# Triangular inverses of both head groups on GpSimd, two key tiles ahead of the first chunk, and value centring by a matrix product

## Chip, core and metric

The kernel runs on one core of a Trainium2 chip. The metric is device microseconds of one execution; the median of three executions of the kernel before is 2632.55 us (2632.36 to 2641.84).

The core has five instruction streams that run side by side and meet through semaphores: TensorE (PE in the profile, with its weight loads as PEld), VectorE (DVE), ScalarE (ACT), GpSimd (POOL) and SyncE (SP), which issues the DMAs. Each engine works through its own queue strictly in order. In this kernel TensorE reads SBUF and writes PSUM, and GpSimd works on SBUF alone.

## The reference, cut to what matters

A network of three layers on 512 tokens of width 1024 in fp32. Only the first mixer, a gated delta-rule recurrence with 16 heads of 64 channels, is touched by the change:

```python
def rwkv7_step(S, inp):
    r_t, dec_t, k_t, v_t, kk_t, a_t = inp
    sa = jnp.einsum('bhij,bhj->bhi', S, -kk_t)
    S = (S * dec_t[:, :, None, :] + sa[..., None] * (kk_t * a_t)[:, :, None, :]
         + v_t[..., None] * k_t[:, :, None, :])
    y = jnp.einsum('bhij,bhj->bhi', S, r_t)
    return S, y
...
    _, y = lax.scan(rwkv7_step, S0, seq)
    m = jnp.mean(y, axis=-1, keepdims=True)
    var = jnp.mean(jnp.square(y - m), axis=-1, keepdims=True)
    y = ((y - m) * lax.rsqrt(var + GN_EPS)).reshape(B, T, D) * ln_g + ln_b
    ...
    bonus = (jnp.sum(rh * kh * r_k, axis=-1, keepdims=True) * vh).reshape(B, T, D)
    out = ((y + bonus) * g).astype(h.dtype) @ w_o
```

The mean over a head's 64 value channels is taken off y. The recurrence is linear in v, so the kernel takes that mean off v before the recurrence instead. The cross attention that follows needs keys and values of a 256-token memory (`mem`), for layer 0 and, later, for layer 1.

## The kernel before, in words

Activations are kept with features on partitions and 512 tokens on the free axis, as eight tiles of 128x512. Weights stream from HBM through two raw buffers (`wraw`, line 41 on) in one fixed order, given by `rw_keys` and its fellows. Most are split into a high and a low part (ScalarE copy, line 63; VectorE or GpSimd subtraction, line 64) and used in three fp32r products (lines 221 to 223). The layer-1 memory keys are not split: one fp32 product each (line 219), straight out of the raw buffer, which is held until the last of the eight products of a tile.

The recurrence is computed in chunks of 64 tokens. The eight feature tiles are two groups of four (g = 0 and 1), and a group is worked off in eight chunks. For one group:

- `key_norms(g)` and `decays(g)` make the norms of the keys and the decays; `scaled(p, ...)` for the group's four tiles makes the scaled keys and queries, and the blocks of a 32x32 strictly triangular system into `qall`, which is `inv[g]`. Its products go through the two `aux` banks of PSUM.
- `inverse32(inv[g], outer)` inverts all these triangular systems at once: it transposes `qall` into `al` on VectorE, builds the inverse in `xl`, and transposes back into `qall`. With `outer` (group 0) it does this by 31 rank-one updates on GpSimd, a product (line 1337) and a sum (line 1338) each. Without it (group 1) it works on VectorE in two 16-row halves and a coupling block (lines 1346 to 1361).
- `prepare(g, n)` makes what chunk n needs without the state: products of keys and queries (line 1389), masked by VectorE (1391), transposes (1395), the inverse of the 64x64 system out of the 32x32 ones (lines 1402 to 1416, with one GpSimd product at 1413), and for every even n `values(g, n)`: transposes of v to tokens (1370), the mean over 64 channels (1373, 1374) and its subtraction (1379), the last three on VectorE.
- `advance(g, n, ...)` carries the state through chunk n: products at 1433, 1441, 1444, 1452 and 1470, with ScalarE and VectorE copies between, and one GpSimd product (1465).

`chunks(g, extra)` runs step n as prepare(n), advance(n - 2), extra(n). For group 0, `extra` is `others`, which does the work of group 1 beside it, by the string `BESIDE[n]`: "a" is key_norms and decays of group 1, a digit 4 to 7 is `scaled` of that tile, "i" the inverse of group 1, a letter A to H a `bonus` (two GpSimd products at line 1271, a head sum on TensorE by lines 1083 and 1084, and a row at 1091). `SPARE` says how many steps of the layer-1 memory keys (one product of line 219 a step, 64 in all) each of the three places in `advance` takes. The layer-0 memory keys follow in group 1; the parts that they need are put where the inverse's tiles lay.

The order of each queue is fixed ahead of the run. A planner places the instructions by its own estimate of their times, with program order as the priority among those that it holds ready; `issue_after` adds an order by hand. So an instruction early in the program can be queued behind a later one.

Of the kernel before, what the change touches and what calls it, by code (L numbers as in the profile page):

```python
# [11 lines left out]
ALU = mybir.AluOpType  # L12
# [83 lines left out]
class Net:  # L96
# [945 lines left out]
    def rwkv_masks(self, pool, scratch):  # L1042
# [13 lines left out]
        self.mlt, self.bd32 = z(32, "mlt"), z(64, "bd32")  # L1056
        nc.gpsimd.memset(self.bd32, 0.0)
# [54 lines left out]
    def rwkv(self, g_next, after):  # L1112
# [210 lines left out]
        def inverse32(qall, outer):  # L1323


            fl = lambda t: t.rearrange("p a b -> p (a b)")
            tmp = tp1.tile([P, 4, T], F32, tag="sig", name=self.nm("inv"))
            al = tp1.tile([P, 32, 32], F32, tag="ee", bufs=2, name=self.nm("al"))
            xl, pr = tmp[:, :2].rearrange("p a (b s) -> p (a b) s", s=32), tmp[:, 2:].rearrange("p a b -> p (a b)")
            nc.vector.transpose(fl(al), fl(qall))  # L1330
            nc.gpsimd.memset(xl, 1.0)
            nc.gpsimd.affine_select(out=xl, in_=xl, compare_op=ALU.is_equal, fill=0.0, base=0, pattern=[[1, 32], [-1, 32]], channel_multiplier=0)
            if outer:

                for k in range(31):
                    o = pr[:, : (31 - k) * (k + 1)].rearrange("p (t s) -> p t s", s=k + 1)
                    PT(out=o, in0=bc(al[:, k + 1 :, k : k + 1], [P, 31 - k, k + 1]), in1=bc(xl[:, k : k + 1, : k + 1], [P, 31 - k, k + 1]), op=ALU.mult)  # L1337
                    PT(out=xl[:, k + 1 :, : k + 1], in0=xl[:, k + 1 :, : k + 1], in1=o, op=ALU.add)  # L1338
                nc.vector.transpose(fl(qall), fl(xl))
                return  # L1340

            for t in range(1, 16):
                o = pr[:, : 2 * t * t].rearrange("p (b s k) -> p b s k", b=2, s=t)
                for b in range(2):
                    c = slice(16 * b, 16 * b + t)
                    TT(out=o[:, b], in0=xl[:, c, c].rearrange("p k s -> p s k"), in1=bc(al[:, 16 * b + t : 16 * b + t + 1, c], [P, t, t]), op=ALU.mult)
                for b in range(2):
                    nc.vector.tensor_reduce(out=xl[:, 16 * b + t, 16 * b : 16 * b + t], in_=o[:, b], axis=AX.X, op=ALU.add)

            m = self.t512("u", 3)[:, :256].rearrange("p (t s) -> p t s", s=16)  # L1350
            for s in range(0, 16, 4):
                o = pr[:, : 64 * (16 - s)].rearrange("p (t s k) -> p t s k", t=16, s=4)
                TT(out=o, in0=bc(xl[:, s:16, s : s + 4].rearrange("p k (t s) -> p t s k", t=1), [P, 16, 4, 16 - s]),
                   in1=bc(al[:, 16:, s:16].rearrange("p t (s k) -> p t s k", s=1), [P, 16, 4, 16 - s]), op=ALU.mult)
                nc.vector.tensor_reduce(out=m[:, :, s : s + 4], in_=o, axis=AX.X, op=ALU.add)
            for t in range(0, 16, 4):
                n = t + 4
                o = pr[:, : 64 * n].rearrange("p (t s k) -> p t s k", t=4, s=16)
                TT(out=o, in0=bc(m[:, :n].rearrange("p k (t s) -> p t s k", t=1), [P, 4, 16, n]),
                   in1=bc(xl[:, 16 + t : 20 + t, 16 : 16 + n].rearrange("p t (s k) -> p t s k", s=1), [P, 4, 16, n]), op=ALU.mult)  # L1360
                nc.vector.tensor_reduce(out=xl[:, 16 + t : 20 + t, :16], in_=o, axis=AX.X, op=ALU.add)
            nc.vector.transpose(fl(qall), fl(xl))
# [3 lines left out]
        def values(g, n):  # L1366

            ps = self.mm()
            for j in range(4):
                nc.tensor.transpose(ps[:, j * P : (j + 1) * P], vv[:, 4 * g + j, n * 64 : n * 64 + P], self.ident)  # L1370
            pv = ps.rearrange("p (j h i) -> p j h i", j=4, h=2)
            mean = self.small(8, "mv")
            nc.vector.tensor_reduce(out=mean, in_=ps.rearrange("p (a i) -> p a i", i=64), axis=AX.X, op=ALU.add)
            TS(out=mean, in0=mean, scalar1=1.0 / 64, scalar2=None, op0=ALU.mult)
            mean = mean.rearrange("p (j h) -> p j h", h=2)
            for c in range(2):
                uv = tp.tile([P, 2, 4, 64], F32, tag="uv", bufs=4, name=self.nm("uv"))
                for hh in range(2):
                    TT(out=uv[H[hh], hh], in0=pv[H[c], :, hh], in1=bc(mean[H[c], :, hh : hh + 1], [64, 4, 64]), op=ALU.subtract)
# [123 lines left out]
        inverse32(inv[0], True)  # L1503
# [14 lines left out]
        def others(n):  # L1518

            for c in BESIDE[n] if n < len(BESIDE) else ():  # L1520
# [3 lines left out]
                elif c == "i":  # L1524
                    inverse32(inv[1], False)
# [5 lines left out]
        def spare(i, ins):  # L1531
            with tc.issue_after(ins):
                for _, advance.km in zip(range(SPARE[i]), advance.keys):
                    pass
# [3 lines left out]
        advance.keys = self.memory_keys(1, 1, self.keys1)  # L1538
        chunks(0, others)
# [5 lines left out]
        advance.keys = keys = self.memory_keys(0, 1)  # L1545

# [88 lines left out]
BESIDE = "a", "457", "6F", "Di", "AGCBEH"  # L1635
# [43 lines left out]
def rw_keys():  # L1679
    al = lambda n: [(n, m, 0, KD) for m in range(KD)]  # L1680
    return (al("rw_k")[:6] + [("rw_a1", 0, 0, KD)] + al("rw_k")[6:] + [("rw_a2", 0, 0, KD), ("rw_w1", 0, 0, KD)] + [("rw_g1", j, 0, KD) for j in range(2)]
            + [("rw_w2", 0, 0, 1)] + al("rw_r")[4:] + al("rw_r")[:4] + al("rw_v") + [("rw_w2", 0, 1, 2)] + kv_keys(1)[:KD] + kv_keys(0) + [("rw_g2", j, 0, KD) for j in range(2)] + al("rw_o"))
# [98 lines left out]
```

## Time and profile before

| | |
|---|---|
| median of three executions | 2632.55 us |
| the profiled execution, its time | 2631.13 us |
| its span in the profile | 2629.4 us |
| TensorE busy | 2516.1 us (96%), mean granted clock 0.968 |
| VectorE busy | 1458.8 us (55%) |
| ScalarE busy | 1068.1 us (41%) |
| GpSimd busy | 363.3 us (14%) |

The shares are means over a long run of stages that differ. The stage of the change reaches from about 190 us, where the inverse of group 0 starts, to about 480 us, where the last chunk of group 1 ends. Of that stage the views by windows, by queue in order of time, and by line are read. In a view by windows each engine has its busy time and, in brackets, its instructions; PEclk is the granted clock of TensorE as a share of full speed (2.4 GHz). In an answer by line, three durations with slashes are the least, the median and the largest, in ns.

### The profile page before, as it was taken

How to read it: one execution, taken by the hardware profiler on the slowest of the kernel's cores; microseconds unless marked ns; L12 is line 12 of the kernel's file. 1: busy time of each engine (PE TensorE's matmuls, PEld its weight loads, DVE VectorE, ACT ScalarE, POOL GpSimd, SP SyncE). 2: the span in 40 equal slices, each digit the busy share in tenths (PEclk: the TensorE clock that was granted, in tenths of full speed). 3: DMA queues.
4: the chain of work that ended last, by engine and by line, in shares of the span. 5: the costliest groups of instructions: out<-in, count | busy, mean ns of one | idle time of the engine just before them, and what ended most of it. 6: DMA issues, size and time to landing. Idle time of an engine off the chain costs nothing.

```text
span 2629.4 us, 33965 instructions
## 1 busy us (share of the span) xinstructions
PE 2516.1 (96%) x13560; PEld 1980.9 (75%) x13560; DVE 1458.8 (55%) x2134; ACT 1068.1 (41%) x1717; POOL 363.3 (14%) x362
## 2 busy tenths in 40 slices
PE   6998989899999999999999999999999999999998
PEld 5666767687888888754788888888776778888886
DVE  7673886655577743322564877434324556555522
ACT  7844445534344432412443444333223444333321
POOL 3035532430100001100202000001010000000000
PEclk9998988899999999999999999999998999999999
DMA  3211111332232233442322322332211113222232
GB/s 127 72 49 43 34 50 41 103 104 65 81 104 97 96 92 100 129 114 81 104 65 73 105 96 97 95 90 75 72 65 41 56 37 116 94 95 95 94 96 80
DMA packets 69597, 218.36 MB, mean 83 GB/s; under 512 B 9227, under 2 KB 14748, under 8 KB 69438
## 3 DMA queue, kind: packets, MB, share of 16 engines
q1 hardware_dynamic: 69438, 216.19, 26.2%
q8 instruction: 106, 1.74, 0.3%
q14 instruction: 53, 0.43, 0.1%
HBM read 205.69 MB, written 2.10 MB: 79 GB/s over the span
## 4 chain that ended last, share of the span: by engine, by line
PE 84%; DVE 9%; ACT 2%; POOL 2%; issue 2%; DMA 0%; DVEq 0%; POOLq 0%; ACTq 0%
PE mm L221 24%; PE mm L222 24%; PE mm L223 24%; PE aux L614 2%; PE aux L324 1%; PE mm L219 1%; POOL inv L1337 1%; POOL inv L1338 1%; DVE u L1177 1%; ACT wh L63 1%; DVE wl L64 1%; PE mm L1011 1%; DVE h L1307 1%; PE aux L984 0%; PE aux L1005 0%
## 5 line engine op out<-in xcount | busy, mean ns | idle before, releaser
L63 ACT ACTIVATE wh<-wr 128x1024 fp32r<-128x1024 f32 (+5 forms) x382 | 388.0, 1019 | 753.1 <-PE mm L222 585.0
L64 DVE TENSOR_TENSOR wl<-wr,wh 128x1024 fp32r<-128x1024 f32 (+3 forms) x341 | 402.8, 1183 | 261.2 <-ACT wh L63 252.2
L222 PE MATMUL mm<-al,wh 128*128 128x512 f32 x1088 | 428.1, 394 | 2.4 <-DVE al L249 2.4
L221 PE MATMUL mm<-ah,wh 128*128 128x512 f32 x1088 | 427.9, 394 | 0.9 <-ACT wh L63 0.8
L223 PE MATMUL mm<-ah,wl 128*128 128x512 f32 x1088 | 422.7, 390 | 0.5 <-DVE wl L64 0.5
L221 PE MATMUL mm<-bh,wh 128*128 128x512 f32 (+1 forms) x1000 | 396.0, 397 | 0.1
L222 PE MATMUL mm<-bl,wh 128*128 128x512 f32 (+1 forms) x1000 | 393.5, 394 | 0.0
L223 PE MATMUL mm<-bh,wl 128*128 128x512 f32 (+1 forms) x1000 | 392.9, 395 | 0.3 <-DVE wl L64 0.3
L221 PEld LDWEIGHTS mm<-ah,wh 128*128 128x128 f32 x1088 | 204.3, 188 | 51.8 <-ACT wh L63 3.5
L223 PEld LDWEIGHTS mm<-ah,wl 128*128 128x128 f32 x1088 | 204.3, 188 | 46.6 <-DVE wl L64 2.3
L222 PEld LDWEIGHTS mm<-al,wh 128*128 128x128 f32 x1088 | 204.5, 188 | 45.7 <-DVE al L249 3.0
L272 POOL TENSOR_TENSOR acc<-acc,sq 128x512 f32<-128x512 f32 x55 | 88.4, 1608 | 981.5 <-ACT sq L271 981.2
L223 PEld LDWEIGHTS mm<-bh,wl 128*128 128x128 f32 (+1 forms) x1000 | 188.3, 188 | 44.7 <-DVE wl L64 1.2
L221 PEld LDWEIGHTS mm<-bh,wh 128*128 128x128 f32 (+1 forms) x1000 | 188.6, 189 | 42.5 <-issue 1.3
L222 PEld LDWEIGHTS mm<-bl,wh 128*128 128x128 f32 (+1 forms) x1000 | 188.5, 189 | 41.9 <-issue 0.7
L384 DVE TENSOR_TENSOR u<-mm,rs 128x512 f32<-128x512 f32 x132 | 90.5, 688 | 168.0 <-PE mm L223 167.9
L64 POOL TENSOR_TENSOR wl<-wr,wh 128x1024 fp32r<-128x1024 f32 (+2 forms) x41 | 99.2, 2423 | 588.7 <-ACT wh L63 586.4
L369 DVE TENSOR_TENSOR x<-x,mm 128x512 f32<-128x512 f32 x56 | 38.4, 686 | 137.0 <-PE mm L223 137.0
L221 PE MATMUL mm<-mh,wh 128*128 128x512 f32 (+1 forms) x224 | 87.6, 413 | 6.3 <-ACT mh L248 4.7
L222 PE MATMUL mm<-ml,wh 128*128 128x512 f32 (+1 forms) x224 | 91.5, 409 | 1.3 <-DVE ml L249 1.3
L223 PE MATMUL mm<-mh,wl 128*128 128x512 f32 (+1 forms) x224 | 90.1, 405 | 1.0 <-DVE wl L64 1.0
L398 ACT ACTIVATE uy<-uy 128x512 f32<-128x512 f32 x66 | 41.6, 631 | 120.3 <-DVE uy L396 120.2
(492 smaller groups left out, 3986.9 us busy)
## 6 DMA issues: line engine op xcount, KB each, us to landing
wr<-ffn_w_in SPq DMA_DIRECT2D x132, 512.0 KB, 3.4
wr<-ffn_w_out SPq DMA_DIRECT2D x48, 448.0 KB, 3.3
wr<-ffn_w_out SPq DMA_DIRECT2D x24, 512.0 KB, 3.5
wr<-hy_g SPq DMA_DIRECT2D x20, 512.0 KB, 3.4
wr<-kv_k SPq DMA_DIRECT2D x16, 512.0 KB, 3.5
wr<-kv_v SPq DMA_DIRECT2D x16, 512.0 KB, 3.5
wr<-xattn_w_q SPq DMA_DIRECT2D x16, 512.0 KB, 3.4
wr<-xattn_w_o SPq DMA_DIRECT2D x16, 512.0 KB, 3.4
```

What stands on the lines that cost most here:

```text
L63: self.last_hi = self.nc.scalar.activation(out=hi[:r, :c], in_=t[:r, :c], func=AF.Copy).ins
L64: (self.nc.gpsimd if i in W_POOL else self.nc.vector).tensor_tensor(out=lo[:r, :c], in0=t[:r, :c], in1=f32(hi[:r, :c]), op=ALU.subtract)
L219: self.last_mm = mm(out, lhsT=w[0], rhs=x[0], start=first, stop=last).ins
L221: mm(out, lhsT=w[0], rhs=x[0], start=first, stop=False)
L222: mm(out, lhsT=w[0], rhs=x[1], start=False, stop=False)
L223: mm(out, lhsT=w[1], rhs=x[0], start=False, stop=last)
L272: nc.gpsimd.tensor_tensor(out=self.sq, in0=self.sq, in1=s, op=ALU.add)
L324: self.last_bcast = self.nc.tensor.matmul(ps[:, b * P : (b + 1) * P], lhsT=col[:, b : b + 1].to_broadcast([P, P]), rhs=self.ident, start=T ...
L369: self.nc.vector.tensor_tensor(out=self.x[m], in0=self.x[m], in1=ps, op=ALU.add)
L384: nc.vector.tensor_tensor(out=u, in0=ps, in1=rs, op=ALU.mult)
L398: self.last_silu = nc.scalar.activation(out=y, in_=y, func=AF.Silu if l < 2 else AF.Gelu_apprx_tanh).ins
L614: nc.tensor.matmul(ps[32 * g : 32 * g + 32, 4 * e :], lhsT=w[:, 8 * g + e], rhs=t[:, g, : T - 4 * e], start=(e == 0), stop=(e == 7), skip_ ...
```

## The change

`values` replaces the four transposes of an even chunk by four products with a fixed 128x128 matrix `cen`, which is the identity less 1/64 in each of its two diagonal 64x64 blocks. The result has tokens on partitions and the mean already taken off, and ScalarE copies it (four copies of 64x256) where VectorE reduced, scaled and subtracted. `cen` is made once on VectorE.

`inverse32` loses the VectorE form: both groups take the 31 rank-one updates on GpSimd.

Sixteen steps (two tiles) of the layer-1 memory keys are issued ahead of the first chunk, and the three places in `advance` take 2, 2, 2 in group 0 instead of 3, 3, 2. Two weight tiles of the keys are moved ahead of the second half of `rw_w2` (which `decays(1)` uses) in the order of the weight DMAs. `BESIDE` has `scaled` of tile 4 in step 0, tiles 5, 6 and 7 in step 1, the inverse in step 2 ahead of bonus F, and D alone in step 3.

```diff
+        self.cen = z(P, "cen")
+        nc.vector.tensor_copy(self.cen, self.ident)
+        for h in range(2):
+            r = slice(64 * h, 64 * h + 64)
+            nc.vector.tensor_scalar(out=self.cen[r, r], in0=self.cen[r, r], scalar1=1.0 / 64, scalar2=None, op0=ALU.subtract)
...
-        def inverse32(qall, outer):
+        def inverse32(qall):
...
-            if outer:
-                for k in range(31):
-                    o = pr[:, : (31 - k) * (k + 1)].rearrange("p (t s) -> p t s", s=k + 1)
-                    PT(out=o, in0=bc(al[:, k + 1 :, k : k + 1], [P, 31 - k, k + 1]), in1=bc(xl[:, k : k + 1, : k + 1], [P, 31 - k, k + 1]), op=ALU.mult)
-                    PT(out=xl[:, k + 1 :, : k + 1], in0=xl[:, k + 1 :, : k + 1], in1=o, op=ALU.add)
-                nc.vector.transpose(fl(qall), fl(xl))
-                return
-            for t in range(1, 16):
...
-                nc.vector.tensor_reduce(out=xl[:, 16 + t : 20 + t, :16], in_=o, axis=AX.X, op=ALU.add)
+            for k in range(31):
+                o = pr[:, : (31 - k) * (k + 1)].rearrange("p (t s) -> p t s", s=k + 1)
+                PT(out=o, in0=bc(al[:, k + 1 :, k : k + 1], [P, 31 - k, k + 1]), in1=bc(xl[:, k : k + 1, : k + 1], [P, 31 - k, k + 1]), op=ALU.mult)
+                PT(out=xl[:, k + 1 :, : k + 1], in0=xl[:, k + 1 :, : k + 1], in1=o, op=ALU.add)
             nc.vector.transpose(fl(qall), fl(xl))
...
-                nc.tensor.transpose(ps[:, j * P : (j + 1) * P], vv[:, 4 * g + j, n * 64 : n * 64 + P], self.ident)
+                mmul(ps[:, j * P : (j + 1) * P], lhsT=vv[:, 4 * g + j, n * 64 : n * 64 + P], rhs=self.cen, start=True, stop=True)
             pv = ps.rearrange("p (j h i) -> p j h i", j=4, h=2)
-            mean = self.small(8, "mv")
-            nc.vector.tensor_reduce(out=mean, in_=ps.rearrange("p (a i) -> p a i", i=64), axis=AX.X, op=ALU.add)
-            TS(out=mean, in0=mean, scalar1=1.0 / 64, scalar2=None, op0=ALU.mult)
-            mean = mean.rearrange("p (j h) -> p j h", h=2)
...
-                    TT(out=uv[H[hh], hh], in0=pv[H[c], :, hh], in1=bc(mean[H[c], :, hh : hh + 1], [64, 4, 64]), op=ALU.subtract)
+                    copy(uv[H[hh], hh], pv[H[c], :, hh])
...
-                for _, advance.km in zip(range(SPARE[i]), advance.keys):
+                for _, advance.km in zip(range(spare.n[i]), advance.keys):
...
+        for _ in zip(range(16), advance.keys):
+            pass
+        spare.n = 2, 2, 2
         chunks(0, others)
...
+        spare.n = SPARE
...
-BESIDE = "a", "457", "6F", "Di", "AGCBEH"
+BESIDE = "a4", "567", "iF", "D", "AGCBEH"
...
-            + [("rw_w2", 0, 0, 1)] + al("rw_r")[4:] + al("rw_r")[:4] + al("rw_v") + [("rw_w2", 0, 1, 2)] + kv_keys(1)[:KD] + kv_keys(0) + [("rw_g2", j, 0, KD) for j in range(2)] + al("rw_o"))
+            + [("rw_w2", 0, 0, 1)] + al("rw_r")[4:] + al("rw_r")[:4] + al("rw_v") + kv_keys(1)[:2] + [("rw_w2", 0, 1, 2)] + kv_keys(1)[2:KD] + kv_keys(0) + [("rw_g2", j, 0, KD) for j in range(2)] + al("rw_o"))
```

## Rows read from the trace of the kernel before

**Rows 1.** By windows: length, PE, PEld, DVE, ACT, POOL, clock, DMA share, GB/s.

```profile
230.00:240.00 10.00, 1.73 (x33) 1.26 (x32) 6.62 (x16) 3.12 (x8) 7.48 (x18) 0.72 0.00 0
240.00:260.00 20.00, 17.46 (x104) 12.91 (x105) 7.55 (x15) 11.64 (x21) 1.67 (x3) 0.59 0.00 1
260.00:300.00 40.00, 35.29 (x501) 27.81 (x500) 30.93 (x48) 18.98 (x51) 20.64 (x18) 0.81 0.06 18
300.00:310.00 10.00, 9.80 (x181) 7.87 (x177) 9.84 (x16) 4.02 (x10) 9.63 (x8) 1.00 0.11 44
310.00:376.00 66.00, 53.06 (x602) 40.38 (x603) 63.72 (x134) 32.32 (x74) 26.46 (x22) 0.91 0.13 41
396.00:480.00 84.00, 79.32 (x1051) 65.31 (x1048) 54.76 (x96) 45.67 (x104) 24.15 (x17) 0.90 0.12 39
```

**Rows 2.** Timeline of TensorE: start, us, instructions, wait before and its releaser.

```profile
238.78 0.64 PE L1406 MATMUL mm<-xb,am 32*32 32x32 f32 x16 [5.45 <-DVE xb L1402]
278.61 3.72 PE L219 MATMUL mm<-mn,wr 128*128 128x256 f32 x16
385.68 0.44 PE L1406 MATMUL mm<-xb,am 32*32 32x32 f32 x16
```

**Rows 3.** By window, the inverse's tiles alone: PE, PEld, DVE, POOL, clock, DMA.

```profile
310.00:376.00 66.00, 2.69 (x48) 1.77 (x48) 36.09 (x82) 4.03 (x4) 0.91 0.13 41
```

**Rows 4.** Timeline of VectorE: around the two inverses.

```profile
197.53 1.40 DVE L64 TENSOR_TENSOR wl<-wr,wh 128x1024 fp32r<-128x1024 f32 x1 [2.93 <-PE aux L436]
236.96 1.25 DVE L1339 STREAM_TRANSPOSE inv<-inv 128x1024 f32<-128x1024 f32 x1 [3.21 <-POOL inv L1338]
310.76 1.25 DVE L1330 STREAM_TRANSPOSE al<-inv 128x1024 f32<-128x1024 f32 x1
370.86 1.24 DVE L1362 STREAM_TRANSPOSE inv<-inv 128x1024 f32<-128x1024 f32 x1
```

**Rows 5.** Timeline of GpSimd: first, disturbed, undisturbed and last update of group 0.

```profile
194.68 0.26 POOL L1337 TENSOR_TENSOR inv<-al,inv 128x31 f32<-128x31 f32 x1 [0.76 <-DVE al L1330]
197.93 1.32 POOL L1337 TENSOR_TENSOR inv<-al,inv 128x135 f32<-128x135 f32 x1
232.79 0.42 POOL L1337 TENSOR_TENSOR inv<-al,inv 128x135 f32<-128x135 f32 x1
236.68 0.25 POOL L1338 TENSOR_TENSOR inv<-inv 128x31 f32<-128x31 f32 x1
```

**Rows 6.** By line: `values` on VectorE, a ScalarE copy of like shape, transposes and products.

```profile
L1373 DVE TENSOR_REDUCE mv<-mm x8: 673/678/691, 230.7 to 453.3; 128x8 f32<-128x512 f32 x8
L1379 DVE TENSOR_TENSOR uv<-mm,mv x32: 374/422/428, 231.7 to 455.7; 64x256 f32<-64x256 f32 x32
L1117 ACT ACTIVATE uv<-chain x16: 379/379/381, 251.1 to 479.6; 64x256 f32<-64x256 f32 x16
L1370 PE MATMUL mm<-ident,vv x32: 272/273/421, 229.1 to 452.2; 128*128 128x128 f32 x32
L1289 PE MATMUL aux<-lcum,sig x64: 272/275/585, 129.5 to 296.6; 128*128 128x130 f32 x64
```

**Rows 7.** Timeline of ScalarE: split of the moved weight, and the sigmoid of `decays(1)`.

```profile
216.35 0.62 ACT L63 ACTIVATE wh<-wr 65x512 fp32r<-65x512 f32 x1
256.31 2.06 ACT L1250 ACTIVATE sig<-mm 128x512 f32<-128x512 f32 x4
```

**Rows 8.** By line: the other GpSimd work of the stage, and VectorE's state product.

```profile
L1271 POOL TENSOR_TENSOR sq<-sq,h x16: 1262/1274/2718, 300.8 to 365.8; 64x512 f32<-64x512 f32 x16
L1413 POOL TENSOR_TENSOR xinv<-inv,bd x16: 844/857/1365, 238.4 to 454.5; 128x256 f32<-128x256 f32 x16
L1465 POOL TENSOR_TENSOR st<-st,fdec x12: 613/622/671, 297.0 to 476.6; 128x256 f32<-128x256 f32 x12
L1461 DVE TENSOR_TENSOR uv<-st,fdec x24: 417/422/1418, 295.9 to 476.0; 64x256 f32<-64x256 f32 x24
```

**Rows 9.** By line, VectorE from 310 to 376 us: the bonus split, count and mean.

```profile
L249 DVE TENSOR_TENSOR u<-sq,u 128x512 fp32r<-128x512 f32 x8 | 5.6, 699 | 0.1
```

More of the change, by code (lines that the diff above doesn't have):

```diff
@@ L1342, in inverse32 @@
-            for t in range(1, 16):
[L1343 to L1360, printed above, removed]
-                nc.vector.tensor_reduce(out=xl[:, 16 + t : 20 + t, :16], in_=o, axis=AX.X, op=ALU.add)
+            for k in range(31):
+                o = pr[:, : (31 - k) * (k + 1)].rearrange("p (t s) -> p t s", s=k + 1)
+                PT(out=o, in0=bc(al[:, k + 1 :, k : k + 1], [P, 31 - k, k + 1]), in1=bc(xl[:, k : k + 1, : k + 1], [P, 31 - k, k + 1]), op=ALU.mult)
+                PT(out=xl[:, k + 1 :, : k + 1], in0=xl[:, k + 1 :, : k + 1], in1=o, op=ALU.add)
@@ L1502, in rwkv @@
         xv = mix(3, mp)
-        inverse32(inv[0], True)
+        inverse32(inv[0])
         project("rw_v", xv, lambda m, ps: copy(vv[:, m], ps))
@@ L1524, in others @@
                 elif c == "i":
-                    inverse32(inv[1], False)
+                    inverse32(inv[1])
                 elif c in "ABCDEFGH":
```

## The prediction

> **What bounds the kernel now.** I read the page first: TensorE is busy for 96% of the span, so over the whole run a gain can only come where TensorE is idle or runs at a low granted clock. Second, the windows of the stage that the change touches [rows 1]. The reader is to see four things. From 230 to 240 us TensorE is busy for 1.73 of 10 us. From 240 to 260 us it is busy for 17.5 of 20 us, but at a granted clock of 0.59, near the lower of its two levels. From 300 to 376 us VectorE is busy for 73.6 of 76 us, TensorE for 62.9: here VectorE is the bound. From 396 to 480 us (most of group 1's chunks) TensorE is the bound, with 79.3 of 84 us. Third, the queues in order of time, to see what holds each of these. The hole at 230 us ends when the first product that needs group 0's inverse starts at 238.78, after a wait of 5.45 us [rows 2], and that inverse ran on GpSimd from 194.68 to 236.93 [rows 5]. The full VectorE is the inverse of group 1: from 310 to 376 us the instructions on its tiles take 36.1 of VectorE's 63.7 us [rows 1, 3], between the transposes at 310.76 and 370.86 [rows 4]. The first product that needs it starts at 385.68 [rows 2].
>
> So two things are for sale: the first inverse's hole with the slow clock after it, and a VectorE-bound stretch of some 75 us. I count from the transposes back (line 1339, later 1362), since they mark the inverse's end.
>
> **The change part by part.**
>
> *The start of group 1's preparation.* Two key tiles, 16 products, cost 3.72 us at full clock [rows 2]. They come out of VectorE-full steps and lie in the hole, where TensorE has nothing else: cost nothing, hidden by the wait for the inverse. They don't shorten that wait, but they leave less idle time ahead of 240 us. If the clock stays up, the 17.5 us at 0.59 would be 10.3 us at full clock, so up to 7.1 us; at worst it falls all the same: 0. I take 3, since 3.7 us fills under half of the hole of 8.3 us. The sigmoids of `decays(1)` (now at 256.31 [rows 7]) and all `scaled` after them move by that. Tile 4 and tile 6 one step earlier in the program change only the priority: 0 to 1, and I take 1. The moved weight: its raw buffer now comes free only after the first key tile's products, so its load and its ScalarE split (216.35, some 40 us ahead of the sigmoid [rows 7]) move to about 238 us. Its cover is the 40 us; without it `decays(1)` waits, and its sigmoids are late by what the load is late. I take 0.
>
> *Values.* On VectorE an even chunk loses 0.68 us of reduction, about 0.15 of scaling and four subtractions of 0.42: 2.5 us [rows 6], eight times, 20 us in all. ScalarE gains four copies, 0.38 us each by a copy of the same size out of PSUM [rows 6]: 1.5 us a time, where it is busy for 36 of 76 us between 300 and 376 [rows 1]: hidden. Two of these chunks lie among `scaled` and the chunks between 260 and 310 us. VectorE is full only at the end of that, so I take 4 of the 5 us (2 to 5). TensorE: a transpose takes 273 ns, an fp32 product with as many rows and two more columns 275 ns [rows 6]. So 32 products for 32 transposes cost nothing (0 to 2 us, should they differ by a fifth). The Trainium skill speaks against this edit: "TensorE: Matmul & The Clock Gate", section Terms, gives the transpose mode as four times faster for FP32. By it each product would cost 0.8 us more, an estimate of 26 us in all, half of it in the TensorE-bound group 1. The two rows side by side show no such factor, and I go by them.
>
> `cen` costs three small VectorE instructions at the start of the run, under 1 us by the reduction's 0.68 us for a larger tile [rows 6]; taken as 0.
>
> *Where the second inverse starts.* Now line 1330 starts at 310.76 [rows 4]. Less 3, 1 and 4 us: 302.8 (range 297 to 310). The first update follows some 1.5 us after: 304.3.
>
> *How long it takes on GpSimd.* In group 0: 42.2 us for 62 updates [rows 5], about 0.68 us each with the gaps. That ran nearly alone; the new place is crowded. First, VectorE. An update of 135 elements took 1.32 us where a VectorE subtraction of two SBUF tiles (1.40 us, started at 197.53) ran beside it, and 0.42 where none did [rows 4, 5]. Now eight bonus splits of 0.70 us [rows 9] and about ten state products of 0.42 (up to 1.42 beside GpSimd work) [rows 8] run in that time. That is 9.8 us of such VectorE work, some of it beside idle gaps: I take 5 (0 to 10). This is also what the Trainium skill says ("SBUF — State Buffer", section SBUF: two separate sides): a VectorE instruction with two SBUF inputs and a GpSimd instruction that reads SBUF lock each other out for a whole instruction. The rows agree, 0.9 us for one of 1.40, and by the rule alone the term would be the upper end, 10.
>
> Second, GpSimd's own queue: 16 bonus products of 1.27 us (20.4 us in all), which start at 300.8, four products of line 1413 at 0.86, five of line 1465 at 0.62 [rows 8]. The last two are 6.5 us and belong to the chain of the chunks, so they must get in. Does the planner let the bonuses in between two updates? On VectorE it did just that with the old inverse, whose 32 us of work was spread over 60 us [rows 3, 4]. I take 12 of the 16, 15.3 us (0 to 20.4). Sum: 42.2 + 5 + 15.3 + 6.5 = 69 us, so the inverse ends at 304.3 + 69 = 373.3, against 370.9 now. It gains nothing by itself: 2.4 us later. What is queued behind it on GpSimd are lines 1413 and 1465 of each chunk; both have most of a step until they are used, and one update is at most 1.5 us, so I take no delay of the chain.
>
> *What the free VectorE gives.* From the transpose back to the first product that needs it, now 370.86 to 385.68: 14.8 us [rows 2, 4], since VectorE and TensorE still have the last chunks of group 0 before them. In group 0, with both engines free, it was 236.96 to 238.78: 1.8 us [rows 2, 4]. With some 42 us (32 of inverse, 10 of values) off VectorE, the chunks of group 0 should be done before 373 us, so I take 1.8 us, a gain of 13.0. Also, TensorE's 13 idle us between 310 and 376 [rows 1] can take work that now stands after 376 (the state-free half of group 1's first chunks, parts of `norms(0)`); against it, TensorE that has run dry restarts group 1 at a lower clock, as after 240 us. I take +3 net (-3 to +8). Values and keys in group 1: VectorE is not the bound there: 0 to 2, taken as 1.
>
> *Sum:* 13.0 - 2.4 + 3 + 1 = 14.6 us. After 480 us nothing changes but its place. From the profiled execution's 2631.13 us (1.7 us outside the span) that is 2616.5; the median is 1.4 us higher, so 2618 us.
>
> **The rivals.**
>
> *The inverse runs free (faster still).* If the planner lets only the chain's 6.5 us in, the updates end at about 303 + 42 + 6.5 + 2 = 354 us, and group 0's own chunks become the bound. They end just ahead of 385.68 now [rows 2]; less TensorE's 13 idle us [rows 1] and the 8 us of the earlier start that is 365. Gain: 21, plus 3 and 1: 25 us, 2608; with the upper ends of the clock (4 more), of the net term (5) and of group 1 (1) it is 35, 2598. For it: the inverse stands before all but a few bonuses in the program. Against it: the spread over 60 us on VectorE.
>
> *GpSimd becomes the bound (slower).* All bonuses in between (20.4), the full 10 us of lock-out, and GpSimd's queue waiting at each product of line 1465 for a chain that on the chip lags the planner's estimate, some 2 us each, 10 in all: 89 us from 304 on, the inverse ends at 393. Gain 13.0 - 22 + 4 = -5, 2637 to 2638. It decides from an inverse end of about 388 us on; at 401 it is slower by over 0.5%. For it: line 1271 stretches to 2.72 and line 1461 to 1.42 at worst [rows 8]. Against it: GpSimd is busy for only 26.5 of 66 us there [rows 1], 4 of them in the tiles of the inverse.
>
> *The keys don't fill the hole.* They need the last memory tile and two banks until the row of norms is there; if they are queued behind product 1406, the hole and the slow clock stay, 3 us are lost: 2621.
>
> *The products with `cen` are slower than transposes.* At four times 273 ns [rows 6] each costs 0.82 us more; the 16 of group 1, where TensorE is the bound, cost 13 us and eat the gain: 2631. (That is the page's factor above; against it stand the two rows.)
>
> **How the numbers follow.** A measurement of this kernel tells about 0.5%, 13 us, from no change. The forecast (with the third rival): 0.60, its own range 2608 to 2626, so about half of it is over 13 us. The free inverse 0.23; GpSimd as the bound 0.14, half of it within 0.5%; products at four times 0.03. Faster by over 0.5%: 0.30 + 0.23 = 0.53. Slower: 0.07. Within: 0.30 + 0.07 + 0.03 = 0.40. The range takes in both outer cases but their tails: 2597 (35 us gained, as above) to 2639 (the GpSimd-bound case and a little).
>
> **What would show it.** TensorE from 230 to 240 us busy for over 5 us, and 240 to 260 at a clock above 0.7; line 1330 of group 1 at 300 to 306 us; its 62 updates over 60 to 75 us with bonus products between; VectorE from 310 to 370 at under 70%; the transpose back near 373 and the first product of line 1406 of group 1 within 4 us of it; TensorE's products with `cen` at 270 to 280 ns. The prediction is wrong if the updates run in one piece in some 48 us, if group 0's chunks outlast the inverse, or if group 1's chunks take longer from their first product to their last than now, 385.68 to about 480 [rows 2, 6].

## The result, and the profile after

The changed kernel takes 2652.11 us (median of 13 executions, 2646.22 to 2657.28) against 2634.83 us for the kernel before on the same chip: a ratio of 1.0060 with a 95% interval of 1.0046 to 1.0074. (The ratio is an estimate from all executions of both kernels and not the quotient of the two medians, here and in the table below.) It is 0.6% slower, some 16 us. Forecast were 2618 us and at most 2639.

The windows of the changed kernel, columns as in [rows 1]:

```profile
230.00:240.00 10.00, 6.18 (x42) 5.17 (x40) 3.99 (x9) 3.00 (x6) 7.55 (x17) 0.96 0.20 66
240.00:260.00 20.00, 16.84 (x153) 13.29 (x153) 10.62 (x20) 14.56 (x29) 1.46 (x2) 0.84 0.10 29
...
310.00:376.00 66.00, 59.71 (x769) 45.35 (x769) 39.28 (x58) 39.89 (x86) 54.95 (x69) 0.95 0.15 52
376.00:396.00 20.00, 5.81 (x82) 4.92 (x84) 7.80 (x14) 5.38 (x16) 11.60 (x20) 0.50 0.09 29
396.00:480.00 84.00, 75.90 (x890) 61.99 (x887) 44.28 (x70) 44.18 (x105) 19.12 (x14) 0.83 0.10 33
```

Up to 376 us this is what the change is for: the hole at 230 us is mostly filled, the clock after it is 0.84 instead of 0.59, VectorE falls from 63.7 to 39.3 us between 310 and 376, and TensorE does 59.7 us of work there instead of 53.1 [rows 1]. Then, from 376 to 396, TensorE is busy for 5.8 of 20 us, at half clock. Before, that stretch was full:

```profile
376.00:396.00 20.00, 18.71 (x242) 14.58 (x241) 14.43 (x29) 10.27 (x23) 4.03 (x3) 0.96 0.32 106
```

And from 396 to 480 it is busier than its number of records explains: 890 in 75.9 us at a clock of 0.83, where before it got through 1051 in 79.3 at 0.90.

TensorE in order of time, around the two holes:

```profile
227.49 5.00 PE L219 MATMUL mm<-mn,wr 128*128 128x256 f32 x22
232.32 0.50 PE L436 MATMUL aux<-ones,sq 128*128 128x1 f32 x4
232.69 2.40 PE L219 MATMUL mm<-mn,wr 128*128 128x256 f32 x10
...
240.77 1.19 PE L324 MATMUL aux<-ident,mcol 128*128 128x128 f32 x4 [4.59 <-DVE mcol L310]
...
370.82 1.07 PE L1410 MATMUL chain<-uv,am 64*64 64x64 f32 x16 [0.47 <-ACT uv L1123]
388.37 0.64 PE L1383 MATMUL mm<-xb,am 32*32 32x32 f32 x16 [16.47 <-DVE xb L1379]
```

Line 1383 is line 1406 of before. TensorE has nothing left at 371.9 us and waits 16.47 us for the inverse of group 1. That inverse lies between these two transposes on VectorE (line 1335 was 1330, line 1343 was 1339):

```profile
313.41 1.25 DVE L1335 STREAM_TRANSPOSE al<-inv 128x1024 f32<-128x1024 f32 x1
...
386.63 1.25 DVE L1343 STREAM_TRANSPOSE inv<-inv 128x1024 f32<-128x1024 f32 x1 [14.41 <-POOL inv L1342]
```

and GpSimd's queue shows what lies among its updates (1341, 1342): bonus products (1277), and in the tail a weight split (64):

```profile
314.73 0.25 POOL L1341 TENSOR_TENSOR inv<-al,inv 128x31 f32<-128x31 f32 x1 [1.03 <-DVE al L1335]
315.06 1.49 POOL L1277 TENSOR_TENSOR sq<-sq,h 64x512 f32<-64x512 f32 x1
...
318.26 2.63 POOL L1277 TENSOR_TENSOR sq<-sq,h 64x512 f32<-64x512 f32 x2 [0.35 <-ACT sq L1274]
...
376.67 2.34 POOL L64 TENSOR_TENSOR wl<-wr,wh 128x1024 fp32r<-128x1024 f32 x1 [0.98 <-ACT wh L63]
...
386.35 0.25 POOL L1342 TENSOR_TENSOR inv<-inv 128x31 f32<-128x31 f32 x1
```

So two things are to be explained: a second inverse that ends 15.8 us later than before (386.63 against 370.86 [rows 4]), and group 1's chunks, which take longer. I measure those from the first state step of group 1 on VectorE (line 1461 of before) to the last: 396.22 to 475.57 before, 79.4 us; 402.05 to 490.36 after, 88.3 us. By that last state step the stage ends 14.8 us later. What follows it takes 2153.8 us in the profile before and 2158.0 after. Over the profiles of all 18 kernels of this study, one execution each, it takes from 2148 to 2162 us, so a few us between two profiled spans say nothing of the stage.

### The profile page after: what moved, and what is told of

It is laid out like the page before. It is cut to its first block, busy times and chain, and to the rows that moved or that the text cites. A ratio compares the mean times of both kernels' runs of the same rounds, so it can differ in the third digit from the quotient of the medians.

```text
span 2648.4 us, 33991 instructions
## 1 busy us (share of the span) xinstructions
PE 2522.1 (95%) x13592; PEld 1987.1 (75%) x13592; DVE 1424.9 (54%) x2013; ACT 1080.5 (41%) x1749; POOL 397.0 (15%) x424
## 4 chain that ended last, share of the span: by engine, by line
PE 87%; DVE 6%; ACT 3%; POOL 2%; issue 1%; DMA 1%; DVEq 0%; POOLq 0%; ACTq 0%
PE mm L223 24%; PE mm L221 24%; PE mm L222 24%; PE aux L614 2%; PE mm L219 1%; PE aux L324 1%; POOL inv L1342 1%; POOL inv L1341 1%; ACT wh L63 1%; DVE wl L64 1%; PE mm L1366 1%; PE mm L1011 1%; DVE h L1313 1%; PE aux L984 0%; PE aux L1005 0%
```

## The experiments

Three theories stood at first: Q, the GpSimd queue delays the inverse; V, the values edit costs the time; K, the keys do. When V had the loss, it was split into P (the products), S (the place of the copies in ScalarE's queue) and O (a lighter VectorE queue lets the planner put other work ahead of the chain). All runs in one table; a ratio is to executions of the kernel before on the same chip. The columns behind the ratio are in us and come from the one profiled execution of each kernel: the starts of the last state step of group 0, of the transpose back of group 1's inverse and of the first state step of group 1, and the length of group 1's steps from the first start to the last.

| kernel | median us | ratio to before (95%) | group 0 ends | inverse back | group 1 starts | its length |
|---|---|---|---|---|---|---|
| before | 2632.70 to 2635.39, by chip | | 372.4 | 370.9 | 396.2 | 79.4 |
| changed | 2652.11 | 1.0060 (1.0046 to 1.0074) | 360.8 | 386.6 | 402.1 | 88.3 |
| e1 inverse | 2632.85 | 0.9983 (0.9970 to 0.9997) | 360.8 | 375.9 | 393.3 | 81.1 |
| e2 values | 2649.63 | 1.0054 (1.0037 to 1.0070) | 376.5 | 369.4 | 404.3 | 89.9 |
| e3 keys | 2634.21 | 0.9990 (0.9975 to 1.0005) | 365.9 | 381.5 | 399.5 | 79.4 |
| e4 changed, bonus on VectorE | 2632.78 | 0.9989 (0.9972 to 1.0006) | 362.4 | 368.3 | 386.1 | 85.9 |
| e5 products | 2633.74 | 0.9994 (0.9983 to 1.0006) | 377.1 | 377.9 | 404.3 | 76.8 |
| e6 copies | 2651.98 | 1.0064 (1.0045 to 1.0084) | 375.8 | 371.9 | 402.5 | 87.2 |
| e7 changed, old values | 2638.06 | 1.0009 (0.9994 to 1.0024) | 358.1 | 381.2 | 396.6 | 76.0 |
| e8 inverse, bonus on VectorE | 2631.14 | 0.9989 (0.9976 to 1.0002) | 372.4 | 370.2 | 397.6 | 80.6 |
| e9 extra copies | 2641.49 | 1.0010 (0.9992 to 1.0028) | 366.9 | 371.5 | 394.4 | 78.6 |
| e10 changed, copies on VectorE | 2640.98 | 1.0024 (1.0012 to 1.0036) | 361.3 | 384.9 | 400.3 | 85.6 |
| e11 values, group 0 only | 2639.68 | 1.0027 (1.0012 to 1.0041) | 376.3 | 369.2 | 407.6 | 80.7 |
| e12 e10 and e4 | 2630.04 | 0.9987 (0.9974 to 1.0000) | 361.6 | 373.6 | 388.1 | 81.6 |
| e13 values, late copies | 2639.01 | 1.0008 (0.9993 to 1.0023) | 371.7 | 370.5 | 399.9 | 77.2 |
| e14 changed, late copies | 2637.69 | 0.9999 (0.9986 to 1.0013) | 361.2 | 384.2 | 404.8 | 76.8 |
| e15 values, copies on VectorE | 2638.72 | 1.0009 (0.9993 to 1.0025) | 373.8 | 372.6 | 398.7 | 82.3 |
| e16 e14 and e4 | 2616.87 | 0.9922 (0.9906 to 0.9939) | 360.4 | 366.3 | 382.6 | 75.1 |

### The parts by themselves (e1 to e3), and the queue relieved (e4)

e1, the inverse alone:

```diff
-                    inverse32(inv[1], False)
+                    inverse32(inv[1], True)
```

> The kernel before with one edit: group 1 takes the rank-one updates on GpSimd too; all else stands. Theory Q (GpSimd's queue: the updates share it with 16 bonus products and the chunks' own products, the inverse ends late, TensorE runs dry, and group 1 then starts at the low clock): the second transpose back at 382 to 392 us (370.9 before), TensorE idle for over 8 us ahead of the first product of line 1406 of group 1, the time 10 to 22 us over before. Rival V (the centring product and its ScalarE copies cost the time): within 5 us of before. Rival K (the keys ahead of the first chunk cost it): within 5 us of before.

Ratio 0.9983: the move alone costs nothing. The inverse ends 5.0 us later, but the chunks of group 0 end 11.6 us earlier, and group 1 starts 3 us earlier. Theory Q as the only cause falls.

e2, the values edit alone (the lines of `cen` and of `values` from the diff, nothing else):

> The kernel before with the values alone changed: product with cen and ScalarE copies, no mean on VectorE. Theory Q: 0 to 6 us faster, since the VectorE-full stretch loses some 5 to 10 us of work and nothing else changes. Rival V: 8 to 18 us slower, with ScalarE waits ahead of chain products or products with cen that take clearly over 275 ns. Rival K: as Q.

Ratio 1.0054, 14 us: nearly the whole loss. e3, the keys alone (the 16 steps ahead of the chunks, 2, 2, 2 in `advance`, the weight order; the old `BESIDE`):

> The kernel before with the keys alone changed: 16 steps ahead of the first chunk, 2, 2, 2 beside the chunks, and the two weight tiles moved ahead of the second half of rw_w2. Theory Q: 0 to 5 us faster; TensorE busy for over 5 of the 10 us from 230, the clock from 240 to 260 over 0.75, but VectorE stays the bound of group 0's chunks, so most of it is not kept. Rival V: as Q. Rival K: 8 to 18 us slower.

No change. Line 1330, the start of the second inverse, comes at 319.45 us in its profile, 8.7 us later than before: the keys don't bring it forward. That they push it back isn't shown, since it comes at 318.23 in e5 and 321.40 in e8, which leave the keys alone.

e4, the changed kernel with the bonus products off GpSimd:

```diff
-                PT(out=c3(s[r]), in0=c3(s[r]), in1=ka[p][r, :, hh], op=ALU.mult)
+                TT(out=c3(s[r]), in0=c3(s[r]), in1=ka[p][r, :, hh], op=ALU.mult)
```

> The changed kernel with the 16 bonus products on VectorE (0.7 us each or less by the neighbouring rows) instead of GpSimd. Theory Q: the updates lose the 16 x 1.3 = 21 us between them, the transpose back comes at 362 to 369 us instead of 386.6, the hole of 16.5 us on TensorE shrinks under 6 us, and the time falls by 16 to 26 us against the changed kernel, to 0 to 12 us under before. Rivals V and K: the inverse ends earlier too, but the time stays 8 us or more above before.

The inverse ends at 368.25 instead of 386.63, group 1 starts 16 us earlier, and the ratio falls from 1.0060 to 0.9989, some 19 us. So the queue does cost time in the changed kernel, where group 0's chunks end early; the loss of V and the loss of Q stand side by side. Group 1's steps stay long, at 85.9 us.

### What of the values edit costs (e5 to e8)

e5, products with the identity where the transposes were, mean and subtraction on VectorE as before:

```diff
-                nc.tensor.transpose(ps[:, j * P : (j + 1) * P], vv[:, 4 * g + j, n * 64 : n * 64 + P], self.ident)
+                mmul(ps[:, j * P : (j + 1) * P], lhsT=vv[:, 4 * g + j, n * 64 : n * 64 + P], rhs=self.ident, start=True, stop=True)
```

> The kernel before, with the 32 transposes of v replaced by 32 fp32 products with the identity; the mean and its subtraction stay on VectorE. Theory P (an fp32 product is two passes of TensorE, a transpose one): 32 records become 64; an even chunk's four take 1.05 to 1.16 us instead of 0.66 at full clock and 1.9 instead of 1.06 at half clock, so 0.4 to 0.9 us more, eight times: 3 to 7 us slower than before. Theory S (the loss of the values edit comes from the copies that stand in ScalarE's queue, not from TensorE): within 1 us of before. If the product alone carries the whole loss, 14 us slower.

Line 1370 has 64 records now, each as long as one transpose (median 275 ns; [rows 6]), so a product is two records. The 3 to 7 us that P expected lie outside the interval (4.5 us faster to 1.6 slower): P falls as the cause.

e6 keeps the transposes and leaves the centring out, so that its result isn't the reference's:

```diff
-                    TT(out=uv[H[hh], hh], in0=pv[H[c], :, hh], in1=bc(mean[H[c], :, hh : hh + 1], [64, 4, 64]), op=ALU.subtract)
+                    copy(uv[H[hh], hh], pv[H[c], :, hh])
```

> The kernel before, with the transposes kept; the mean of v and its subtraction are left out and ScalarE copies the four blocks of an even chunk in their place (the output lacks the centring). Theory S: most of the 14 us of the values edit stays, so 7 to 14 us slower than before, and group 1's chunks take 86 to 90 us from the first state step to the last instead of 79. Theory P: no slower than before, 0 to 5 us faster, because VectorE loses 20 us of work, and group 1's chunks take about 79 us.

Ratio 1.0064, 17 us, a little over what S expected: with fewer VectorE instructions and no product, the loss is all there. e7, the changed kernel with the old `values`:

> The changed kernel with the old values path (transposes, mean and subtraction on VectorE); keys ahead, inverse on GpSimd and the new order of the group 1 work stay. If the values edit is the cause of the loss: 12 to 16 us faster than the changed kernel, so 2633 to 2637 against 2634 for the kernel before. If the GpSimd queue with the bonus products among the updates is a cause of its own: the inverse still ends near 386 us, the hole of 10 us or more ahead of group 1's first product stays, and the time stays over 2640.

The loss goes (1.0009), though the inverse still ends at 381.2 us and TensorE waits 11.68 us ahead of group 1's first product. Against the expectation for a queue that is a cause of its own, the time is not over 2640. e8, e1 with the edit of e4:

> The kernel before, with the inverse of group 1 on GpSimd and the bonus products on VectorE; old values, old keys, old order. If the parts add up (the changed kernel gained 19 us by the bonus products on VectorE, and the values edit costs 14): 2616 to 2622, 13 to 19 us faster than before. Rival: VectorE, which keeps the means and now has the bonus products too, is full again between 300 and 376 us and the inverse's early end is of no use: 2629 to 2635, no change.

The time is the rival's, within 0.5% of before, but not for its reason: VectorE is not full (51.1 of the 66 us from 310). With the old values path and the bonus products on it group 0's chunks end at 372.4 us, as before, behind the inverse at 370.2, so its early end is of no use.

### Load or place (e9 to e12)

e9 adds four ScalarE copies of nearly the same size to the kernel before, into a tile that nobody reads:

```diff
+                dm = tp.tile([P, 4, 60], F32, tag="dm", bufs=1, name=self.nm("dm"))
+                for hh in range(2):
+                    copy(dm[H[hh]], pv[H[c], :, hh, :60])
```

> The kernel before with its values path untouched, and four more ScalarE copies (64x240) of the transposed v in every even chunk, into a tile that nobody reads. Theory S (the copies stand in ScalarE's queue ahead of the copies am and v of the chain, so TensorE waits for v): 5 to 17 us slower than before, group 1's chunks 84 to 90 us from the first state step to the last instead of 79. Rival O (the loss comes from the lighter VectorE queue: the planner then puts other VectorE work between the two masks of a chunk): within 3 us of before, group 1's chunks 76 to 81 us.

Its twelve executions lie from 2624.99 to 2644.03 us, so the ratio says little beyond "under 8 us". The trace says more. ScalarE in an even chunk of group 1 (line 1411 is the copy v that the chain waits for, dm are the added copies):

```profile
423.55 0.55 ACT L1411 ACTIVATE v<-mm 32x128 f32<-32x128 f32 x2
...
427.53 0.74 ACT L1117 ACTIVATE dm<-mm 64x240 f32<-64x240 f32 x2
...
429.61 0.75 ACT L1117 ACTIVATE dm<-mm 64x240 f32<-64x240 f32 x2 [0.36 <-DVE uv L1379]
```

The added copies stand behind v, not ahead of it as I had meant, and group 1 takes 78.6 us. So in group 1 four more copies on ScalarE, behind v, are no load that counts. What is left of S is their place.

e10, the changed kernel with VectorE copies, and e12, the same with the edit of e4:

```diff
-                    copy(uv[H[hh], hh], pv[H[c], :, hh])
+                    nc.vector.tensor_copy(uv[H[hh], hh], pv[H[c], :, hh])
```

> The changed kernel, with the four copies of the centred values on VectorE instead of ScalarE; everything else as changed. Theory S: the loss goes, 2633 to 2639, as with the old values path, and group 1's chunks take 76 to 81 us. Rival O: VectorE is still lighter by some 0.8 us an even chunk, so a part of the loss stays, 2642 to 2652, and group 1's chunks take 84 to 90 us.

> The changed kernel, with the copies of the centred values on VectorE and the bonus products on VectorE. If the two repairs add up (the bonus products on VectorE brought 19 us, the old values path 14, of which at most the 16 us of loss and the hole of 16 us ahead of group 1 can be had): 2616 to 2628. If they repair the same loss: 2630 to 2636.

e10 repairs some 10 of 16 us, which is between what S and O expected, and group 1's steps still take 85.6 us, as O expected. One mechanism of O is to be seen in it. VectorE from the fifth to the sixth state step of group 1 (line 1368 are the two masks of a chunk, line 249 is a split for the layer-0 memory keys):

```profile
469.05 0.69 DVE L1368 TENSOR_TENSOR am<-mm,mzr 128x512 f32<-128x512 f32 x1 [0.66 <-PE mm L1366]
470.00 1.80 DVE L249 TENSOR_TENSOR h<-u,h 128x256 fp32r<-128x256 f32 x1 [0.25 <-ACT h L248]
471.73 0.68 DVE L1368 TENSOR_TENSOR am<-mm,mzr 128x512 f32<-128x512 f32 x1
```

and TensorE beside it:

```profile
472.46 0.44 PE L1383 MATMUL mm<-xb,am 32*32 32x32 f32 x16 [1.62 <-DVE am L1368]
```

The split stands between the two masks, and TensorE waits 1.62 us for the second. In e14 the split stands behind both; from state step to state step it is 9.1 us there (465.96 to 475.09) and 12.3 here (467.13 to 479.42). e12 is even with before.

e11, the values edit in group 0 only:

```diff
-                nc.tensor.transpose(...)
+                (mmul(..., rhs=self.cen, ...) if g == 0 else
+                 nc.tensor.transpose(...))
...
+            if g: (mean as before)
+                    if g: (subtraction as before)
+                    else: copy(uv[H[hh], hh], pv[H[c], :, hh])
```

> The kernel before, with the products with cen and the ScalarE copies in group 0 only; group 1 keeps transposes, mean and subtraction. If the loss arises in group 1's chunks, where TensorE is the bound: 0 to 5 us slower than before, group 1's chunks 76 to 81 us. If it arises in group 0 as well (group 1 started 8 us late with the full edit): 6 to 10 us slower.

About half of the loss (1.0027): group 1's steps are short again, but it starts 11 us late, as in e2 (8 us). The windows of e2 there, and the product of TensorE ahead of them:

```profile
375.00:380.00 5.00, 2.94 (x19) 2.21 (x20) 4.94 (x12) 1.85 (x5) 0.91 (x2) 0.66 0.24 92
380.00:385.00 5.00, 5.00 (x34) 3.52 (x33) 1.61 (x2) 0.64 (x1) 0.00 (x0) 0.50 0.35 105
385.00:390.00 5.00, 5.00 (x27) 3.32 (x26) 1.17 (x2) 2.02 (x3) 0.84 (x1) 0.50 0.00 0
390.00:395.00 5.00, 4.90 (x61) 3.97 (x59) 3.51 (x6) 2.64 (x6) 0.00 (x0) 0.97 0.10 20
```

```profile
377.06 0.45 PE L1435 MATMUL chain<-uv,am 128*64 128x64 f32 x2 [3.05 <-DVE uv L1463]
```

Group 0's last state step (376.49) is late, TensorE waits 3.05 us for it, and from 380 to 390 it works without a gap at half clock, where before the clock was 1.00: 5 us of loss behind a wait of 3.

### The place itself (e13 to e16)

In `prepare`, `values(g, n)` is called ahead of the 32x32 products. These runs call it at the end:

```diff
-            if n % 2 == 0:
-                values(g, n)
...
                     copy(am[R[hh], hh, :, :64], zr[H[hh], p0 : p0 + 4, 0, ch])
+            if n % 2 == 0:
+                values(g, n)
             return am, tm, uvs.pop((g, n)), xinv
```

e13 is e2 with this, e14 the changed kernel with this; e15 is e2 with VectorE copies; e16 is e14 with the edit of e4.

> The kernel before with the values edit alone, but with values(g, n) called at the end of prepare, so that the four ScalarE copies are queued behind the copies v and am of the same chunk (in the values edit alone, 14 us slower, they stand ahead of them). Theory S: most of the loss goes, 2630 to 2638. Rival O: VectorE is just as light and the loss stays, 2643 to 2652.

> The changed kernel with values(g, n) called at the end of prepare. Theory S: 8 to 16 us faster than the changed kernel, 2634 to 2642. Rival O: within 4 us of the changed kernel, 2646 to 2656.

> The kernel before with the products with cen, and four VectorE copies where the mean and its subtraction were; ScalarE as before, VectorE lighter by some 0.8 us an even chunk. Theory S: no slower than before, 0 to 5 us faster. Rival O: 4 to 10 us slower, as the changed kernel with VectorE copies is (6 us).

> The changed kernel with values(g, n) called at the end of prepare and the bonus products on VectorE. With theory S, and the 19 us that the bonus products on VectorE brought in the changed kernel: 2618 to 2628, the fastest of all. Rival O: like the changed kernel with the bonus products on VectorE alone, 2630 to 2636.

The place counts in both pairs: 1.0054 becomes 1.0008, and 1.0060 becomes 0.9999, with the same instructions on the same engines. The late call moves more than the copies, though: TensorE's products for `values` go behind the 32x32 products, and the planner orders VectorE anew. In the early place TensorE's part cost nothing that could be measured in e5. VectorE's order isn't separated: e15, with the copies off ScalarE, is at 1.0009 (its interval holds no change and 6 us, and so doesn't choose between S and O), e10 at 1.0024, and group 1's steps take 82.3 and 85.6 us in their profiles, against 77.2 and 76.8 in e13 and e14. So S is the larger part of the loss by the times, and how much of the rest is O stays open. The same even chunk of group 1, ScalarE first, in the changed kernel:

```profile
431.81 0.36 ACT L1123 ACTIVATE gg<-chain 128x256 f32<-128x256 f32 x1
432.91 1.54 ACT L1123 ACTIVATE uv<-mm 64x256 f32<-64x256 f32 x4 [0.73 <-PE mm L1351]
434.48 0.41 ACT L1123 ACTIVATE am<-zr 64x256 f32<-64x256 f32 x1
434.92 0.56 ACT L1385 ACTIVATE v<-mm 32x128 f32<-32x128 f32 x2
```

and in e14 (v is line 1382 there):

```profile
433.79 0.36 ACT L1123 ACTIVATE gg<-chain 128x256 f32<-128x256 f32 x1
434.18 0.41 ACT L1123 ACTIVATE am<-zr 64x256 f32<-64x256 f32 x1
434.62 0.56 ACT L1382 ACTIVATE v<-mm 32x128 f32<-32x128 f32 x2
...
436.98 1.56 ACT L1123 ACTIVATE uv<-mm 64x256 f32<-64x256 f32 x4 [0.39 <-PE mm L1351]
```

TensorE in the changed kernel, then in e14:

```profile
431.71 1.16 PE L1351 MATMUL mm<-cen,vv 128*128 128x128 f32 x8
...
435.24 0.91 PE L1389 MATMUL mm<-inv,v 32*32 32x32 f32 x16 [1.13 <-ACT v L1385]
...
447.77 0.44 PE L1410 MATMUL chain<-uv,am 128*64 128x64 f32 x2 [1.47 <-DVE uv L1438]
```

```profile
434.94 0.91 PE L1386 MATMUL mm<-inv,v 32*32 32x32 f32 x16
435.79 1.16 PE L1351 MATMUL mm<-cen,vv 128*128 128x128 f32 x8
```

Ahead of v, the four copies hold ScalarE until 434.45, and TensorE waits 1.13 us for v; behind it, there is no wait. TensorE's waits for v over all of group 1's steps (total, number, longest), in the changed kernel and in e14:

```profile
PE mm L1389 <- ACT v L1385: 3.0, 4, 1.1
```

```profile
PE mm L1386 <- ACT v L1382: 0.6, 3, 0.2
```

In e10 and e15 it is 0.6 us as well: there the steps are long without a wait for v. Later in this step the changed kernel's chain meets VectorE work of `norms(0)` as well (the wait of 1.47 us for line 1438). The step takes 18.3 us (427.21 to 445.50) against 11.5 in e14 (429.20 to 440.74), which is 6.7 of the 11.5 us between the two kernels' steps. Over all of group 1's steps, first the changed kernel, then e14:

```profile
402.05:490.36 88.31, 80.21 (x992) 66.44 (x991) 46.70 (x74) 46.99 (x110) 21.26 (x15) 0.86 0.10 34
```

```profile
404.76:481.59 76.83, 72.76 (x992) 60.20 (x989) 45.32 (x74) 47.02 (x110) 21.07 (x15) 0.93 0.13 40
```

The same 992 records of TensorE take 80.2 us at a clock of 0.86 and 72.8 at 0.93; idle are 8.1 and 4.1 us. Of the 11.5 us between the two, 4.0 are idle time, 2.4 of them waits for v, and 7.5 are longer busy time at the lower clock. Since e14's group 1 starts 2.7 us later, its stage ends 8.8 us earlier in these two profiles; the rest of the 16 us between the two ratios lies behind the stage, where profiles differ by that much in any case.

e16 is the fastest kernel of the study, just ahead of what S expected: 0.9922 of before, 20 us faster. The inverse there, TensorE's first product behind it, and the window that was the hole:

```profile
366.25 1.23 DVE L1343 STREAM_TRANSPOSE inv<-inv 128x1024 f32<-128x1024 f32 x1
```

```profile
368.06 0.44 PE L1380 MATMUL mm<-xb,am 32*32 32x32 f32 x16 [0.60 <-DVE xb L1376]
```

```profile
376.00:396.00 20.00, 16.23 (x253) 13.06 (x251) 8.76 (x15) 13.52 (x32) 6.37 (x4) 1.00 0.19 65
```

The four kernels with the whole change form a square: 1.0060 (as made), 0.9999 (late copies), 0.9989 (bonus on VectorE), 0.9922 (both). Late copies bring 0.0061 and 0.0067, the relieved queue 0.0071 and 0.0077: the two losses, some 16 and 19 us, add up within the intervals (some 4 us either way for each ratio), and what is left without them is a gain of 20 us.

## Why the prediction was wrong, step by step

Forecast were 14.6 us gained, and some 16 were lost. Two steps account for 29 of these 31 us: the second inverse ended 13.3 us later than forecast, since its start didn't come forward, and the values edit, whose ScalarE copies were put down as hidden, cost some 16 us at its place in the queues. e14, which has the first loss without the second, bears the sum out: 14.6 less 13.3 is 1.3 us, and it is even with before.

- *Values, the step that failed most.* "ScalarE gains four copies, ... where it is busy for 36 of 76 us ...: hidden." A share of busy time says nothing of the place in the queue: the copies stand ahead of v and am, on which the chain waits. Issued there, the values edit cost some 14 to 17 us (e2, e6, and the changed kernel against e14); issued behind, nothing that could be measured (e13, e14). With the copies on VectorE in the early place, 10 and 12 of these us come back (e10, e15), so most of the loss goes with the copies' place on ScalarE; the rest is open between O and noise. The prediction asked of GpSimd what is queued behind a new instruction, and did not ask it of ScalarE.
- *Products for transposes.* The two rows of 273 and 275 ns [rows 6] are records, not products. Line 1351 has 64 records for 32 products:

```profile
L1351 PEld LDWEIGHTS mm<-cen,vv x64: 186/192/338, 243.5 to 464.4; 128*128 128x128 f32 x64
L1351 PE MATMUL mm<-cen,vv x64: 272/275/582, 243.9 to 464.5; 128*128 128x128 f32 x64
```

  So an even chunk's products take 1.16 us where the four transposes of line 1372 take 0.66 in the same step (429.90). In this the price of nothing was wrong, but not by enough to be measured (e5). The Trainium skill ("TensorE: Matmul & The Clock Gate", Terms) has the direction right; its factor of four is two here in records, and 1.8 in these times. The rival built on it (2631) is not what happened.
- *The keys.* The same mistake: the x16 of [rows 2] are 8 products (line 219 has 128 records for the 64 products), so two tiles cost 7.4 us (5.00 and 2.40 above), not 3.72. They fill the hole, and 240 to 260 us runs at 0.84, as forecast. But the hole still ends with the inverse: what VectorE makes of the row of norms (line 436, now 2.9 us later at 232.32) is queued behind the inverse's transpose, and TensorE waits for it until 240.77, where before it got it at 240.07. And most of chunk 0's own products, which lay ahead of the hole (lines 1395, 1370 and 1433 of before), now lie behind it. The sigmoids come at 256.15 instead of 256.31 [rows 7]: of the 3 us nothing arrives.
- *Where the second inverse starts.* Forecast 302.8, range 297 to 310; it is 313.41. With the keys alone it is 319.45 (e3) and with the values alone 313.80 (e2), and in none of the 18 profiles does it come ahead of the 310.76 of before: none of the 3, 1 and 4 us that were to bring it forward was there. The moved `scaled` steps were not tried alone. The moved weight's split came at 235.52, and no engine is seen to wait for it, as forecast.
- *How long it takes on GpSimd.* Forecast 69 us from 304.3; from 314.73 to 386.60 it is 71.9. 13 of the 16 bonus products lie in it with 16.8 us (forecast 12 and 15.3), the chain's products with 5.5 (6.5) and the weight split with 2.3 (not in the sum); the updates and the gaps are the other 47.3 (42.2 + 5). So the size was right nearly term by term, which is not luck; the start was 10.4 us off, and so the end was 13.3 us late. The bonus products among the updates, in the sum at their right size, are what e4 and e16 won back: some 19 us.
- *What the free VectorE gives.* Transpose back to first product: 1.7 us, forecast 1.8. Group 0's chunks are done long before (last state step 360.8). The mechanism was right, and e16 shows its gain; but with the inverse at 386.6 it turns into TensorE's wait of 16.47 us with a restart at a clock of 0.50. The prediction had this loss in a net term whose worst end was 3 us.
- *The rivals.* GpSimd as the bound, with a chance of 0.14, is what happened to the inverse, short of its end of 393, for which it gave 5 us slower. e14, which has this loss without the other, ends the inverse at 384.2 and is even with before (0.9999): by the rival's own sum that end would be a gain of some 4 us, at the edge of the interval (0.9986). Nothing among the rivals had the ScalarE queue, so the time of the changed kernel lies outside the range. The last sentence, that group 1's chunks may not take longer than 385.68 to about 480, named the place: first product to last they took 388.37 to 495.5, 107.1 us, against 385.68 to 480.7 before, 95.0. That sign was right, by a mechanism that the prediction didn't have.

## What to carry to other kernels

Work that is moved to a half-idle engine is priced by its place in that engine's queue as well as by the engine's share: find what stands behind it and who waits for that, and if it isn't urgent, issue it behind the urgent work. A stretch that two chains end (here the inverse and group 0's chunks) pays only when both end earlier; look at both before selling the time between. And count records against the program's instructions before a duration of one record is taken as a price.

## What the runs showed of the hardware that was not expected

- An fp32 product shows as two records and two weight loads, a transpose as one of each; the weight load of a product's pass takes 192 ns in the median, that of a transpose 140, in the line of before:

```profile
L1370 PEld LDWEIGHTS mm<-ident,vv x32: 138/140/230, 229.0 to 452.1; 128*128 128x128 f32 x32
```

- A short wait can cost more than its length, and by different amounts. In e2 a wait of 3.05 us is followed by 10 us of work without a gap at a granted clock of 0.50, the lower of the two levels (380 to 390). In the kernel before, waits of 1.20, 0.81 and 0.60 us between 371 and 374.4 are followed by some 4 us at 0.57 and 0.58 (374 to 378) and then by 1.00. Between the changed kernel's group 1 steps and e14's, the longer busy time at the lower clock is nearly twice the longer idle time (7.5 against 4.0 us).
